# Another way to spread silu(c) over the partitions, in the first microseconds of a hybrid mixer layer

## The chip, the cores and the metric

The kernel runs on one core of a Trainium2 chip. The metric is device time in microseconds (us) of one execution. A core has five engines that run beside each other and meet through semaphores: TensorE (PE, matrix products), VectorE (DVE), ScalarE (ACT), GpSimd (POOL) and SyncE (SP), and 16 DMA engines that move the data that SP, ACT and POOL ask for.

## The reference

One decoder layer on 1024 tokens of 1024 features, all in fp32. Cut to what matters here:

```python
c_act = silu(c)                                   # c has 1024 values
mod = c_act @ mod_w + mod_b                       # 1024 x 3072
shift, scale, gate = split(mod, 3)
h = rmsnorm(x, norm_g) * (1 + scale) + shift
u = h @ w_in                                      # 1024 x 5120: five parts
cv, cg, cs, lx, ls = split(u, ...)
y_conv = (silu(layernorm(conv31(cv * sigmoid(cg)))) @ pw2_w + pw2_b) * silu(cs)
y_lru = linear_scan(gates of conv4(lx)) * silu(ls)
x = x + (1 + gate) * (concat(y_conv, y_lru) @ w_out)
return rmsnorm(x, final_g)
```

Nothing of h can be computed before scale is known, and scale needs silu(c) times a third of mod_w.

## The kernel before

The features lie on the 128 partitions, in 8 tiles k = 0 to 7; the tokens lie along the free dimension. Large products are made of fp32r parts: an operand is cast to a high part (ACT) and the rest is formed by a subtraction (DVE, or POOL for some weights), and three products of such parts stand for one product: high times high, high times low, low times high.

**The opening.** All small vectors (biases, gains, c) come in one tile V, loaded by SP before everything else (L413). ACT makes cs = silu(c), 128 x 8 values. DVE needs silu(c) as a row that lies on every partition, since it forms scale as sums over the free dimension of mod_w's transposed rows. PE spreads it: `spread_c` (L724) multiplies, for each k, an identity with the column k of cs broadcast as weights, so that 128 columns of c_row receive the 128 values of that column on all partitions. Two PSUM tiles c_row0 and c_row1 hold four columns' worth each. These are fp32 products. Before and after them PE does filler products with `ones` (`idle_mm`, L721; IDLE = 12 in all, IDLE0 = 4 of them ahead of the spread). The two PSUM tiles come from the pool "mm" of three, of which the first output tiles also take theirs.

`first_dot` (L819) forms the first 128 values of scale from the two halves of c_row directly, in two products with modw on DVE, and adds the first half's sum into b1; after each, ACT copies that half of c_row to the buffer sc in SBUF, which later dots read. Then DVE forms gs = (sum + b) * norm_g, and with it uh = x * gs as the high part and ul as the low part.

**The first tiles.** Four output tiles of W_in (FIRST) are computed with k outermost, as x, mod_w and w_first arrive: for each k, a load of mod_w, of the first weights (`fraw`), of x; a dot; the cast of fraw to fhi (ACT), flo (DVE); uh and ul; products "first" on PE. The token statistics (squares of x) are summed beside it, and at the end PE sums them (token_stats), ACT takes the root, DVE the reciprocal st, PE spreads it with the identity, and ACT copies that to rbc, which scales the four tiles when DVE takes them out of PSUM (first_u). One half of the fourth tile has no room in PSUM at first and is computed afterwards ("late"), in the buffer of 512 columns that the other half of that tile leaves. The next three tiles (NEXT; "ps" and then DVE's "next") use the same unscaled uh and ul; their weights are cast on ACT to whi and completed on POOL as wlo. Beside this DVE works on shift (dots with mod_w, then "shift") and on its share of the bias (fsum).

**What sets the order.** Every operation is recorded with an engine, a cost, a priority, what it reads and writes. `Plan.order` simulates the five engines with these costs, picks on each free engine the ready operation of lowest priority number, and so writes one order by hand for each queue; the hardware then runs each engine in that order, with waits where data is needed. An operation's changed cost or priority can thus move others. Lines called helpers below: L345 and L353 are all of ACT's copies and activations, L364, L372 and L386 DVE's (and L372 POOL's) operations, L391 SP's loads. Operations called outside the plan (V's load, the identity, the memsets) come first on their engines. SP0 is the time at which the plan lets SP start.

Of the kernel before, what the change touches and what calls it, by code (L numbers as in the profile page):

```python
# [9 lines left out]
F32 = mybir.dt.float32  # L10
F32R = mybir.dt.float32r
AF = mybir.ActivationFunctionType
ALU = mybir.AluOpType

P = 128
D = 1024
T = 1024
KT = D // P
H = 512
# [8 lines left out]
DWW = SCW + KT * STAPS  # L28
# [4 lines left out]
FW = len(FIRST) * P  # L33
# [40 lines left out]
WARM = (2, 1)  # L74
LANDING, MARGIN = 4.0, 2.0
BACKLOG = 6.0
SP0 = 1.0
SPP = 35
PAD = 16
GLO = "DVE"  # L80
# [220 lines left out]
def hymba_layer(ctx: ExitStack, tc: tile.TileContext, xT, vecs, mod_w, w_first, w_in,  # L301
                gate_w, pw2, w_out, out):
    nc = tc.nc
    ctx.enter_context(tc.manual_schedule())
    act, dve, pool, pe, sp = nc.scalar, nc.vector, nc.gpsimd, nc.tensor, nc.sync

    const = ctx.enter_context(tc.tile_pool(name="const", bufs=1))
# [19 lines left out]
    S = Plan(pools)  # L327
# [11 lines left out]
    def ACT(prio, out, in_, func, n=T, bias=None, scale=None, accum=None, r=(), w=(),  # L339
            reserve=0, after=()):  # L340
        kw = {}

        def emit():
            if func == "copy":
                act.copy(out(), in_())  # L345
                return
            if bias is not None:
                kw["bias"] = bias
            if scale is not None:
                kw["scale"] = scale  # L350
            if accum is not None:
                kw["accum_out"] = accum
            act.activation(out=out(), in_=in_(), func=func, **kw)  # L353
        ptr = sum(x is not None and not isinstance(x, float) for x in (bias, scale))
        return S.op("ACT", a_cost(n, ptr) + (0.1 if accum is not None else 0), emit, prio, r, w,
                    table=SETS.get(func), reserve=reserve, after=after)
# [42 lines left out]
    def big_buf(name, dt=F32, parts=1):  # L399
        return S.buf("big", name, dt, parts)  # L400
# [9 lines left out]


    V = const.tile([P, NVEC], F32, tag="V", name="V")
    sp.dma_start(V[:, :DWW], vecs[:, :DWW])  # L413

    def vec(name, t):
        o = OFF[name] + t
        return V[:, o:o + 1]

    ident = const.tile([P, P], F32, tag="ident", name="ident")
    make_identity(nc, ident)  # L420
    ones = const.tile([P, P], F32, tag="ones", name="ones")
    dve.memset(ones, 1.0)
    ones_d = const.tile([P, P], F32, tag="ones_d", name="ones_d")
# [89 lines left out]
    def half(b, i):  # L513
        return part(b, i * H, i * H + H)
# [191 lines left out]

    xt = [big_buf(f"x{k}", parts=4) for k in range(KT)]
    sc = big_buf("sc", parts=2)  # L710
    psf = [mm_tile(f"first{n}", 4) for n in range(3)] + [acc_tile("first3")]
# [5 lines left out]
    cs, ps_c = ctile("cs", KT), [mm_tile(f"c_row{z}") for z in (0, 1)]  # L717
# [3 lines left out]
    def idle_mm():  # L721
        pe.matmul(psb()[:, :P], ones, ones, start=True, stop=True)

    def spread_c(z):  # L724
        for k in range(4 * z, 4 * z + 4):
            pe.matmul(half(ps_c[z], 0)()[:, k % 4 * P:k % 4 * P + P], cs[:, k:k + 1].to_broadcast([P, P]), ident,
                      start=True, stop=True)
    for i in range(IDLE):
        if i == IDLE0:
            for z in (0, 1):  # L730
                spread_op = S.op("PE", 0.11 * KT, lambda z=z: spread_c(z), -130, [("cs", 0)],
                                 [ps_c[z]], columns=2 * P * KT)
        S.op("PE", 0.22, idle_mm, -120, [], [psb], columns=4 * P,
             after=[spread_op] if i >= IDLE0 else [])
    def mod_load(j, prio, after=(), reserve=0):
# [16 lines left out]
    def fw_part(b, k, a=0, e=FW):  # L752
        o = (k % 2) * FW
        return lambda: b()[:, o + a:o + e]
# [24 lines left out]
    for i, ld in enumerate(LOADS):  # L779
        p = due[ld] = i - 100.0  # L780
        k = int(ld[1])
        if ld[0] == "s":
            mod_load(KT + k, p, reserve=RES)
        elif ld[0] == "h":
            mod_load(k, p, reserve=RES)
        elif ld[0] in "wW":
            nk = 1 + (ld[0] == "W")
            rw, hi, lo = fw[k - k % 2]
            n, o, js = nk * FW, (k % 2) * FW, range(k % 2, k % 2 + nk)
            keys = lambda b: [(b, j) for j in js]  # L790
            DMA(p, part(rw, o, o + n), lambda k=k, j=nk: w_first[k * P:(k + j) * P, :].rearrange(
                "(p j) f -> p (j f)", j=j), n * P * 4, w=keys(rw))
            for j in range(k, k + nk):
                due[f"w{j}"] = p
                jj = j % 2
                p += 1.5 * (j > k)
                ACT(p, fw_part(hi, j), fw_part(rw, j), "copy", FW, r=[(rw, jj)], w=[(hi, jj)])
                low[j] = SUB(p, "DVE", fw_part(lo, j), fw_part(rw, j), fw_part(hi, j), FW,
                             r=[(rw, jj), (hi, jj)], w=[(lo, jj)])
        else:  # L800
            if ld[0] == "a":
                due["x0"] = p
            for z in {"a": (0,), "b": (1,)}.get(ld[0], (0, 1)[:1 + (k == 0)]):
                x_load(p, xt[k], k, z)
# [30 lines left out]
    for k in range(KT):  # L835
        p = due[f"s{k}"]
# [3 lines left out]
        else:  # L840
            dot(SCALE[k], p, KT + k, [gs_op])
        gs_op = S.op("DVE", 0.2, lambda k=k, a_=a_: dve.scalar_tensor_tensor(
            out=col(gs, k), in0=a_, scalar=col(b1, k), in1=vec("norm_g", k), op0=ALU.add,
            op1=ALU.mult), p, [("macc", KT + k), ("b1", 0)], [("gs", k)], lock=True)
        p = max(p, due[f"x{k}"], due[f"w{k}"])
# [4 lines left out]
        for a, e in START if k < UK else ((0, T),):  # L850
            n = e - a
            hk = halves(x_, a, e)
            if k == 0 == a:
                o = first_u = TS(p, part(uh, a, e), part(x_, a, e), g, None, ALU.mult, n=n,
                       r=hk + [("gs", k)], w=halves(uh, a, e))
            else:
                o = ACT(p, part(uh, a, e), part(x_, a, e), AF.Copy, n, scale=g,
                        r=hk + [("gs", k)], w=halves(uh, a, e))
# [3 lines left out]
                r=hk + halves(uh, a, e) + [("gs", k)], w=halves(ul, a, e)))  # L862
# [3 lines left out]
        for ch, z in ((ch, z) for ch in (0, 1) for z in range(3 if k < ZK else 0)):  # L866
            for i, ps in enumerate(psf):
                if START[ch] in cuts[i]:
                    o = fw_mm(p + 0.1 * ch, ps, i, uh, ul, k, START[ch:ch + 1], z=z)
                    last_u[k, i, ch] = o  # L870
        for ch, (a, e) in enumerate(START):
            for i, ps in enumerate(psf):
# [3 lines left out]
                o = fw_mm(q, ps, i, uh, ul, k, ((a, e),))  # L876
# [3 lines left out]
    for k in range(KT):  # L880
        p = SQP + k
# [3 lines left out]
        for i, j in SQPAIR.get(k, ()):  # L885
            a, b = sqs[i], sqs[j]
# [21 lines left out]
    for a, e in START:  # L908
# [3 lines left out]
                         w=halves(rbc, a, e))  # L912
# [7 lines left out]
    for k in range(KT):  # L920
        p = due[f"h{k}"]
# [3 lines left out]
            out=col(shift, k), in0=a_, in1=vec("mod_shift_b", k), op=ALU.add), p,  # L925
            [("macc", k)], [("shift", k)], lock=True)
        rw = fw[k - k % 2][0]
        if k == 0:
            ACT(p, facc, fw_part(rw, k), AF.Copy, FW, scale=shift[:, k:k + 1],
                r=[(rw, 0), ("shift", k)], w=[(fsum, 0)])  # L930
# [3 lines left out]
        for i, s in enumerate(NEXT):  # L934
            to, rw = part(fsum, FW + i * P, FW + i * P + P), raw[s]
            src = lambda rw=rw, k=k: k3(rw)()[:, k, :]
            if k == 0:
                ACT(p + 5, to, src, AF.Copy, P, scale=shift[:, k:k + 1],
                    r=[(rw, k), ("shift", k)], w=[(fsum, 1)])
            else:  # L940
                STT(p + 5, to, src, shift[:, k:k + 1], to, ALU.mult, ALU.add, P,
                    r=[(rw, k), ("shift", k), (fsum, 1)], w=[(fsum, 1)])
    psx = mm_tile("psbias", 2)

    def shift_mm():
# [5 lines left out]
        w=[("bias", 0)])  # L951

    hh, hl = uhs, uls

    for ch, (a, e) in enumerate(START):
        for k in range(KT):
            p, n = TP + k + HCH * ch, e - a
# [57 lines left out]
    v, c = {}, {}  # L1015
# [210 lines left out]
    for i, (s, ps) in enumerate(zip(FIRST, psf)):  # L1226
        j, p, bi = s[1] % KT, EVP + i, bias[:, i:i + 1]
        t = big_buf(f"first_u{i}", parts=4)
        for a, e in START:
            tk, pk, n = halves(t, a, e), halves(ps, a, e), e - a  # L1230
# [3 lines left out]
            else:  # L1234
                late = acc_tile("late")
                for k in range(KT):
# [3 lines left out]
                   r=[late] + halves(rbc, a, e), w=tk)  # L1240
# [13 lines left out]
    n, started, acc_d = 3, {}, {}  # L1254
    for s in slots[4:]:
# [10 lines left out]
        ps = mm_tile(f"ps{n}")  # L1266
# [5 lines left out]
        for k in range(KT):  # L1272
            o = mm_k(n, ps, s, xh, xl, k, FULL)
# [13 lines left out]
        else:  # L1287
            t = big_buf(f"acc{m}")
            for z in (0, 1)[:1 + (m == 0)]:
                x_load(n - 1, t, m, z, [started[n - 2]])  # L1290
            STT(n + 0.5, t, ps, gate1[:, m:m + 1], t, ALU.mult, ALU.add,
                r=[ps, t, ("gate1", m)], w=[t])
# [7 lines left out]
    begun_pw2, last = [], [started[n - 1], started[n]]  # L1300
    for p in range(KT // 2):
        n = C0 + 2 * p
        w = pair_weights("pw2", p, n, last[:1], last[1:], WPW[p])
        ops, found = next(pair_products(f"pw2_{p}", n, w, v_sets, PW7[p]))
        begun_pw2.append(ops)
        last = [ops[0], ops[3]]
# [22 lines left out]
    acc, n = {}, D0  # L1329
# [163 lines left out]
```

## Time and profile before

| | us |
|---|---|
| median of 3 runs | 735.97 |
| lowest and highest | 735.59 and 736.16 |
| profiled execution, span from first to last instruction | 734.5 |
| PE busy in the span | 725.2 |
| DVE busy | 626.0 |
| ACT busy | 445.7 |
| POOL busy | 139.3 |

The page of the profile gives the profiled execution by its span alone; the median of the runs is 1.5 us longer than that. A busy time counts instructions from start to end; products on PE overlap, so 99% busy does not mean that it does as much as it could, only that it hardly waits. Rows of a timeline give the start in us from the span's start, the length, the engine, the line, the operation with out<-in, the shape and a count; brackets hold the idle time of the engine ahead of it and what ended it.

### The profile page before, as it was taken

The page shows a single profiled execution, that of the slowest core. Times are in us where ns is not written, and L with a number is a line of the kernel's source. Part 1 is how long each engine was busy: PE and PEld are TensorE (multiplying, and loading weights), DVE is VectorE, ACT ScalarE, POOL GpSimd, SP SyncE. Part 2 cuts the span into 40 slices and gives each one's busy share as a digit, 9 for nine tenths or more (in the row PEclk, how much of TensorE's full clock was granted, in tenths as well). Part 3 has the DMA queues.
Part 4 walks back from the last instruction along what each step waited for, and adds up shares of the span by engine and source line. Part 5 has one row for each costly group of instructions (what it writes and reads, how often), then busy time and mean ns, then how long its engine had stood idle before and what let it go on. Part 6 is the DMA issues. An engine that isn't in the chain of part 4 may idle for free.

```text
span 734.5 us, 8866 instructions
## 1 busy us (share of the span) xinstructions
PE 725.2 (99%) x3280; PEld 602.5 (82%) x3280; DVE 626.0 (85%) x834; ACT 445.7 (61%) x564; POOL 139.3 (19%) x125
## 2 busy tenths in 40 slices
PE   9999999999999999999999999999999999999996
PEld 8888888888888887888888888878888888888885
DVE  6999999999569996888598999849699766999756
ACT  7650677556679759957849788524664324565522
POOL 0024012344424222232214111310000000000003
PEclk9999999999999999999999999999999999999998
DMA  9951023458898999899654645634232530523306
GB/s 347 406 217 58 0 87 79 89 115 193 187 211 193 240 250 216 169 232 210 142 112 98 146 85 142 197 133 167 92 115 85 202 115 2 187 93 121 115 1 229
DMA packets 37483, 111.58 MB, mean 152 GB/s; under 512 B 4160, under 2 KB 12864, under 8 KB 37440
## 3 DMA queue, kind: packets, MB, share of 16 engines
q1 hardware_dynamic: 23904, 75.84, 29.7%
q0 software_dynamic: 12528, 34.26, 25.5%
q10 hardware_dynamic: 1008, 0.92, 0.4%
q8 instruction: 25, 0.41, 0.2%
q14 instruction: 18, 0.15, 0.1%
HBM read 64.16 MB, written 12.58 MB: 104 GB/s over the span
## 4 chain that ended last, share of the span: by engine, by line
PE 80%; DVE 12%; issue 3%; ACT 3%; DMA 2%; POOL 0%; DVEq 0%; SPq 0%; ACTq 0%; POOLq 0%
PE ps L489 54%; PE xpw L611 6%; PE xout L611 4%; PE ypw L611 3%; PE out L662 3%; DVE caccs L364 2%; DVE modw L364 2%; PE gate L1171 2%; PE yout L611 2%; PE zpw L611 1%; DVE ul L364 1%; DVE cacc L364 1%; PE zout L611 1%; DVE o L364 1%; DMA oo<-co 1%
## 5 line engine op out<-in xcount | busy, mean ns | idle before, releaser
L489 PE MATMUL ps<-uh,whi 128*128 128x512 f32 x576 | 177.4, 389 | 0.3 <-ACT scs L353 0.3
L489 PE MATMUL ps<-uh,wlo 128*128 128x512 f32 x576 | 177.4, 389 | 0.0
L489 PE MATMUL ps<-ul,whi 128*128 128x512 f32 x576 | 177.4, 389 | 0.0
L489 PEld LDWEIGHTS ps<-uh,whi 128*128 128x128 f32 x576 | 107.9, 188 | 23.0 <-ACT scs L353 0.7
L489 PEld LDWEIGHTS ps<-uh,wlo 128*128 128x128 f32 x576 | 108.1, 188 | 22.6
L489 PEld LDWEIGHTS ps<-ul,whi 128*128 128x128 f32 x576 | 108.1, 188 | 22.4
L345 ACT CAST whi<-raw 128x1024 fp32r<-128x1024 f32 x46 | 48.0, 1047 | 73.7 <-PE ps L489 45.3
L377 POOL DMA_DIRECT2D es<-cq x45 | 41.6, 946 | 124.6 <-ACT cq L353 92.7
L372 POOL TENSOR_TENSOR wlo<-raw,whi 128x1024 fp32r<-128x1024 f32 x16 | 40.1, 2515 | 125.9 <-ACT whi L345 85.1
L353 ACT ACT_TABLE_LOAD x45 | 57.7, 1283 | 4.9 <-DMA oo<-co 3.4
L364 DVE SCALAR_TENSOR_TENSOR cacc<-v,V,cacc 128x511 f32<-128x511 f32 (+14 forms) x75 | 55.8, 744 | 0.5
L364 DVE SCALAR_TENSOR_TENSOR caccs<-v,V,caccs 128x511 f32<-128x511 f32 (+6 forms) x70 | 52.2, 745 | 2.4 <-ACT caccs L353 1.1
L364 DVE SCALAR_TENSOR_TENSOR caccs<-c,wsum,caccs 128x511 f32<-128x511 f32 (+6 forms) x70 | 52.1, 744 | 1.0
L372 POOL TENSOR_TENSOR o<-fin,bc 128x256 f32<-128x256 f32 (+1 forms) x7 | 6.0, 889 | 244.8 <-ACT bc L345 244.8
L377 POOL DMA_DIRECT2D oo<-co x42 | 38.2, 955 | 65.1 <-ACT co L353 23.2
L372 DVE TENSOR_TENSOR wlo<-raw,whi 128x1024 fp32r<-128x1024 f32 x30 | 38.5, 1284 | 9.9 <-ACT whi L345 9.9
L489 PE MATMUL ps<-yh,whi 128*128 128x512 f32 x128 | 40.0, 394 | 0.0
L489 PE MATMUL ps<-yl,whi 128*128 128x512 f32 x128 | 39.5, 390 | 0.0
L489 PE MATMUL ps<-yh,wlo 128*128 128x512 f32 x128 | 39.4, 389 | 0.0
L353 ACT ACTIVATE cq<-v,V 128x511 f32<-128x511 f32 (+14 forms) x45 | 31.8, 707 | 0.0
L364 DVE SCALAR_TENSOR_TENSOR xs<-ps,V,xs 128x1023 f32<-128x1023 f32 (+2 forms) x24 | 30.7, 1277 | 0.0
L364 DVE SCALAR_TENSOR_TENSOR modw<-modw,sc 128x1024 f32<-128x1024 f32 x23 | 30.1, 1311 | 0.0
(334 smaller groups left out, 1449.7 us busy)
## 6 DMA issues: line engine op xcount, KB each, us to landing
raw<-in_w_in_dram SPq DMA_DIRECT2D x36, 512.0 KB, 4.8
modw<-in_mod_w_dram SPq DMA_DIRECT2D x24, 512.0 KB, 8.1
raw<-in_w_out_dram SPq DMA_DIRECT2D x10, 512.0 KB, 4.0
scsd<-scs SPq DMA_DIRECT2D x8, 512.0 KB, 4.2
accd<-acc SPq DMA_DIRECT2D x8, 512.0 KB, 2.8
rawpw<-in_pw_dram SPq DMA_DIRECT2D x8, 512.0 KB, 3.5
scsr<-scsd SPq DMA_DIRECT2D x8, 512.0 KB, 5.8
fin<-accd SPq DMA_DIRECT2D x8, 512.0 KB, 4.8
```

Of the source, the lines that this page charges most:

```text
L345: act.copy(out(), in_())
L353: act.activation(out=out(), in_=in_(), func=func, **kw)
L364: dve.scalar_tensor_tensor(out=out(), in0=in0(), scalar=scalar, in1=in1(), op0=op0, op1=op1, accum_out=accum)
L372: lambda: e.tensor_tensor(out=out(), in0=a(), in1=b(), op=op), prio, r, w,
L377: return S.op("POOL", ISSUE, lambda: pool.dma_start(out(), a(), accum_op=ALU.add), prio, r, w, lag=RATE * n / T, after=after)
L489: pe.matmul(ps()[:, a - off:b - off], k3(lhs)()[:, k, :], rhs[k]()[:, a:b], start=(k == 0 and lhs is wh and rhs is xh and (a - off) % H == 0),
L611: pe.matmul(half(ps, 0)(), half(*lhs)()[:, j * P:j * P + P], half(*rhs)(), start=start and j == 0 and t == 0, stop=j == KT // 2 - 1 and t ...
L662: pe.matmul(ps()[:, a - off:e - off], k3(lhs)()[:, k, :], rhs()[:, i * H + a % H:i * H + a % H + e - a], start=k == KORD[0] and lhs is wh ...
L1171: pe.matmul(ps()[:, c0:c1], lhs()[:, j, :], rhs()[:, c0:c1], start=st == 0, stop=st == 2)
```

## The change

Four things change.

- V is loaded by a DMA that ACT issues, not SP; SP's first DMA is now the first piece of mod_w. The planner's SP0 goes from 1.0 to 0.6.
- The identity is a tile of type fp32r. POOL makes an identity in a large buffer, and DVE copies it. The fp32 uses read the same tile through a view.
- cs is split on DVE into csh (its fp32r cast) and csl (the rest). The spread multiplies the fp32r identity with csh and then with csl, summed in PSUM: 16 fp32r products in place of 8 fp32 products.
- The cast of the first weights (fhi for k = 0) gets the priority -101.5, ahead of ACT's copies of c_row to sc.

```diff
-SP0 = 1.0
+SP0 = 0.6
...
-    sp.dma_start(V[:, :DWW], vecs[:, :DWW])
+    act.dma_start(V[:, :DWW], vecs[:, :DWW])
...
-    ident = const.tile([P, P], F32, tag="ident", name="ident")
-    make_identity(nc, ident)
+    ident_r = const.tile([P, P], F32R, tag="ident", name="ident")
+    ident = ident_r.bitcast(F32)
+    made = big_buf("made")
+    S.op("POOL", 1.0, lambda: make_identity(nc, made()[:, :P]), -150, [], [made])
+    S.op("DVE", 0.2, lambda: dve.tensor_copy(ident_r, made()[:, :P]), -150, [made],
+         [("ident", 0)])
...
+    def two_parts(name, full, r, prio):
+        n = full.shape[-1]
+        hi, lo = (const.tile([P, n], F32R, tag=name + z, name=name + z) for z in "hl")
+        S.op("DVE", 0.15, lambda: dve.tensor_copy(hi, full), prio, r, [(name + "h", 0)])
+        S.op("DVE", 0.15, lambda: dve.tensor_tensor(
+            out=lo, in0=full, in1=hi.bitcast(F32), op=ALU.subtract), prio,
+            [*r, (name + "h", 0)], [(name + "l", 0)], lock=True)
+        return hi, lo
+
+    def spread_two(ps, hi, lo, ks, o):
+        k0 = ks[0]
+        for c, last in ((hi, False), (lo, True)):
+            for k in ks:
+                a = o + (k - k0) * P
+                pe.matmul(ps()[:, a:a + P], c[:, k:k + 1].to_broadcast([P, P]), ident_r,
+                          start=a % H == 0 and not last, stop=last, skip_group_check=True)
...
+    csh, csl = two_parts("cs", cs, [("cs", 0)], -130)
+
     def spread_c(z):
-        for k in range(4 * z, 4 * z + 4):
-            pe.matmul(half(ps_c[z], 0)()[:, k % 4 * P:k % 4 * P + P], cs[:, k:k + 1].to_broadcast([P, P]), ident,
-                      start=True, stop=True)
+        spread_two(lambda: half(ps_c[z], 0)(), csh, csl, range(4 * z, 4 * z + 4), 0)
     for i in range(IDLE):
         if i == IDLE0:
             for z in (0, 1):
-                spread_op = S.op("PE", 0.11 * KT, lambda z=z: spread_c(z), -130, [("cs", 0)],
-                                 [ps_c[z]], columns=2 * P * KT)
+                spread_op = S.op("PE", 0.06 * KT, lambda z=z: spread_c(z), -130,
+                                 [("csh", 0), ("csl", 0), ("ident", 0)], [ps_c[z]], columns=P * KT)
...
-                ACT(p, fw_part(hi, j), fw_part(rw, j), "copy", FW, r=[(rw, jj)], w=[(hi, jj)])
+                ACT(p if j else -101.5, fw_part(hi, j), fw_part(rw, j), "copy", FW, r=[(rw, jj)], w=[(hi, jj)])
```

What the planner makes of it, read from the two programs: ACT begins with V's load, then its first table load; its first cast of fraw comes ahead of both copies to sc. DVE's add of the first half's sum to b1 comes after the second half's product. Some flo, ul and sq operations change places between 16 and 40 us. On ACT the table load for the root comes ahead of fsum, and the first cast of NEXT weights (whi) after the first copy to rbc. On DVE the first_u operations come earlier among shift and fsum, and the softplus steps later. On POOL the wlo of the first NEXT tile is the third operation, not the second. On PE the sums of squares come one group of three products earlier among the "first" products, and the spreading of st moves among them. On SP two mod_w loads change places with weight loads. From about 100 us on the order is the same on every engine.

## Prediction

> **What bounds the kernel now.** I read the page's head first, then the waits of TensorE over the whole span, then the timeline of each engine over the first 60 us.
>
> ```profile
> span 734.5 us, 8866 instructions
> PE 725.2 (99%) x3280; PEld 602.5 (82%) x3280; DVE 626.0 (85%) x834; ACT 445.7 (61%) x564; POOL 139.3 (19%) x125
> ...
> PE token_stats L722 <- DVE ones L422: 1.1, 1, 1.1
> PE finbc L690 <- DVE rs64.5_0_5690 L699: 0.9, 1, 0.9
> PE late L765 <- DVE first_u L372: 0.8, 1, 0.8
> PE ps L489 <- ACT scs L353: 0.3, 1, 0.3
> ```
>
> TensorE (PE) waits four times in 734.5 us, 3.1 us in all. So only three things can move the end: work that PE does before its first useful product, one of these waits, or a new wait. The changed program has the same order on every engine after about 100 us, so I look at the first 60 us and take what PE has gained or lost there as carried to the end.
>
> ```profile
> 1.06 2.08 PE L722 MATMUL token_stats<-ones 128*128 128x128 f32 x8 [1.06 <-DVE ones L422]
> 3.00 3.75 PE L726 MATMUL c_row<-ident,cs 128*128 128x128 f32 x16
> 6.54 2.13 PE L722 MATMUL token_stats<-ones 128*128 128x128 f32 x16
> 8.43 1.17 PE L765 MATMUL first<-uh,fhi 128*128 128x512 f32 x4
> ...
> 41.19 1.84 PE L894 MATMUL token_stats<-ones,sq 128*128 128x1 f32 x16
> 42.89 0.49 PE L765 MATMUL first<-uh,fhi 128*128 128x512 f32 x1
> ```
>
> Columns: start, length, engine, line, tiles, count. The spread c_row is 8 fp32 products, shown as 16 passes: (6.54-3.00)/16 = 0.221 us each. The 16 filler passes after it need (8.43-6.54)/16 = 0.118. Later fp32 passes need (42.89-41.19)/16 = 0.106. So PE begins at half pace; with n filler passes at 0.221 and the rest at 0.106, n is 1.7, and full pace comes near 6.9 us. From 8.43 to 50.45 PE never waits.
>
> **The start, part by part.**
>
> ```profile
> 0.74 0.37 SPq L413 DMA_DIRECT2D V<-in_vecs_dram  x1
> 1.17 0.42 SPq L391 DMA_DIRECT2D modw<-in_mod_w_dram  x1
> ...
> 0.74 1.28 ACT L353 ACT_TABLE_LOAD   x1 [0.74 <-PEq L1485]
> 2.65 0.21 ACT L353 ACTIVATE cs<-V 128x8 f32<-128x8 f32 x1 [0.63 <-DMA V<-in_vecs_dram]
> 5.78 0.21 ACT L353 ACTIVATE sp_u<-sp_u 128x8 f32<-128x8 f32 x1
> 5.90 0.57 ACT L345 COPY sc<-c_row 128x512 f32<-128x512 f32 x1
> 6.36 0.62 ACT L345 CAST fhi<-fraw 128x512 fp32r<-128x512 f32 x1
> ...
> 2.65 0.17 DVE L386 TENSOR_SCALAR b<-V 128x16 f32<-128x16 f32 x1 [1.50 <-DMA V<-in_vecs_dram]
> 6.79 0.69 DVE L364 SCALAR_TENSOR_TENSOR modw<-modw,c_row 128x512 f32<-128x512 f32 x1 [0.82 <-PE c_row L726]
> 7.52 0.22 DVE L842 SCALAR_TENSOR_TENSOR gs<-macc,b,V 128x1 f32<-128x1 f32 x1
> 7.78 0.49 DVE L386 TENSOR_SCALAR uh<-x,gs 128x512 fp32r<-128x512 f32 x1
> ```
>
> V's load. On ScalarE (ACT) it goes ahead of the table load: 0.74+0.37+1.28 = 2.39, before V's landing at 2.65, so the issue is hidden; if V landed before 2.39 it would cost up to the 0.37. SP's other loads start 1.17-0.74 = 0.43 earlier. What V loses by sharing the engines with a 512 KB load is between 0 and 1.28 us (rival below); I take 0, the row as it stands.
>
> Identity. POOL makes it in another buffer, and VectorE (DVE) copies 128x128 in about 0.17 in its 1.50 us idle time: hidden. Without that cover it is 0.17.
>
> Two parts. c_row now waits for one more small DVE operation, csh. One such step, gs to uh, takes 7.78-7.52 = 0.26, so c_row starts at 3.26. The second part, csl, runs under the first four products.
>
> One-pass products. There are still 16, now one per part. What one takes at half pace no row shows.
>
> ```profile
> 11.27 0.84 PE L765 MATMUL first<-uh,fhi 128*128 128x512 f32 x3
> 11.95 0.84 PE L765 MATMUL first<-uh,flo 128*128 128x512 f32 x3
> ...
> 718.14 0.28 PE L662 MATMUL out<-yhb,whi 128*128 128x256 f32 x1
> 719.09 0.28 PE L662 MATMUL out<-yhb,wlo 128*128 128x256 f32 x1
> ```
>
> fp32r products take 0.227 us for 512 columns (0.68/3) and 0.119 for 256 (8 products in 0.95). By that slope 128 columns take 0.065, at half pace (times 0.221/0.118 = 1.9) 0.12. From above, if the 16 weight loads set the pace, 0.221 as today. The nearest rows are the one-pass products, so I take 0.13: c_row is issued from 3.26 to 5.35, not to 6.54. [...]
>
> What follows. The second modw product started 6.79-6.54 = 0.25 after c_row; now 5.60. gs followed 0.73 after that start; now the one-element add to b, hidden before, lies between (0.13 with its wait): 6.46, and uh 6.72. uh led to PE's first product in 8.43-7.78 = 0.65: 7.37. The cast of fraw no longer stands behind a copy of sc and may start at 5.90, where the table loads end, and be done by 6.5. The two copies of sc follow, to about 7.6; PE's second and third product need those buffers, and start after that anyway.
>
> Filler. PE still has 16 filler passes between. From 5.35 to 6.9 it does 7 at 0.221, then 9 at 0.106: 7.87. So fillers set the start: 8.43-7.87 = **0.56 us gained**, and up to 1.06 (7.37) where full pace comes sooner.
>
> Can the rest follow? The loads run 0.43 earlier, and DVE runs 1.06 ahead of its old times. The reordered flo, ul and sq operations between 20 and 40 us cost nothing as long as PE has none to wait for there, as today.
>
> **The middle.**
>
> ```profile
> 49.40 1.05 PE L900 MATMUL token_stats<-ident,st 128*128 128x128 f32 x8
> 51.29 0.50 PE L765 MATMUL late<-uh,fhi 128*128 128x512 f32 x1 [0.84 <-DVE first_u L372]
> 57.79 0.62 PE L489 MATMUL ps<-uh,wlo 128*128 128x512 f32 x2
> ...
> 44.72 0.20 DVE L907 RECIPROCAL st<-st 128x8 f32<-128x8 f32 x1
> 47.34 2.37 DVE L924 TENSOR_TENSOR shift<-macc,V 128x1 f32<-128x1 f32 x1
> 50.56 1.87 DVE L372 TENSOR_TENSOR first_u<-first,rbc 128x512 f32<-128x512 f32 x3
> ...
> 45.78 1.03 ACT L345 CAST whi<-raw 128x1024 fp32r<-128x1024 f32 x1
> 47.52 0.59 ACT L345 COPY rbc<-token_stats 128x512 f32<-128x512 f32 x1 [0.71 <-PE token_stats L900]
> ...
> 46.89 2.81 POOL L372 TENSOR_TENSOR wlo<-raw,whi 128x1024 fp32r<-128x1024 f32 x1 [45.58 <-ACT whi L345]
> 53.09 10.26 POOL L372 TENSOR_TENSOR wlo<-raw,whi 128x1024 fp32r<-128x1024 f32 x4 [3.39 <-DVE first_u L372]
> ```
>
> PE's 0.84 us wait is for the first_u that empties first3's buffer. It starts at 50.56 because a one-column shift took 2.37 us: it began inside POOL's wlo (46.89 to 49.70) and ended with it. In the changed order that cast of whi stands behind rbc, so POOL starts at 47.52+0.59+1.03 = 49.1; and on DVE only two shifts, a 512 fsum, a modw dot and another fsum lie between the reciprocal and first_u: the work that today lies between the starts at 44.72 and 47.34, 2.6 us, and one shift more. In today's clock: ready at 47.4, rbc at 48.1, first0's first_u to 48.7, first3's to 49.4, before PE reaches late at 50.45. **0.84 us gained**, with 1.0 us in hand; the other end is 0.
>
> What is late next: the wlo of the first NEXT tile (ps from 56.89). It was POOL's second wlo and becomes its third. POOL takes 10.26/4 = 2.57 each: 49.1 to 51.9, 54.5, 57.1; PE needs it where it now starts the wlo products, at 57.79-0.84 = 56.95. Wait 0.15, more where DVE holds POOL up; between 0 and 1.0 for a first reading I take **0.3 lost**.
>
> Sum: 0.56+0.84-0.30 = 1.1 us. The span becomes 733.4. The median of the runs, 735.97, lies 1.5 us above the profiled span; I keep that and forecast **734.9 us**. A measurement of this kernel tells about 0.2%, 1.47 us, from no change, so this stands just inside.
>
> **Rivals.**
> More gain: full pace comes within c_row and POOL does not stop PE: 1.06+0.84 = 1.9, 734.1. For it: the moment of full pace is not tied to this work by any row. Against: the profile has it at 6.9.
>
> V late. Today its packets have the engines first. If one 512 KB load passes first, V lands 1.28 later:
>
> ```profile
> 10.33 0.33 SPq L391 DMA_DIRECT2D x<-in_xT_dram  x1
> 11.61 0.33 SPq L391 DMA_DIRECT2D modw<-in_mod_w_dram  x1
> ...
> out_dram<-o ACTq DMA_DIRECT2D x7, 128.0 KB, 2.1
> ```
>
> (SP's issues here come one landing apart.) c_row runs 4.54 to 6.6, the fillers end near 8.5 and ACT's copies, 1.28 later, hold the third product to 8.9: PE about 0.3 later than today; 735.97+0.3-0.84+0.3 = 735.7. Against it: at the end ACT's stores land in 2.1 us beside SP's. [...]
>
> Weight loads bind (0.221 each): c_row ends 6.80, second modw 7.05, PE at 8.82, 0.39 later than today; 735.8.
>
> Half pace lasts: the thinner products do not count as the same activity. If it lasts one more stretch as long as c_row today, 3.5 us, to 10.4, the fillers end at 5.35+3.54 = 8.89 and half of the 1.5 us to 10.4 is lost: PE 1.2 later, 736.6. [...]
>
> Slower: POOL's third wlo. Today its second stood 3.39 us for work of others. If the third stands as long, it ends at 60.5 and PE waits 3.5 us in the first NEXT tile: 735.97-1.4+3.5 = 738.1. It decides from an end past 58.4 (today's clock). Against: two operations now pass first, and its inputs are older by then.
>
> **How the numbers follow.** Forecast 734.9 (own range 734.2 to 735.6) 0.43, of which 0.12 lies under 734.5; more gain 0.26; V late 0.09; weight loads 0.07; half pace 0.05; POOL 0.10. Faster by over 0.2%: 0.12+0.26 = 0.38; slower 0.10; within 0.52. The low end is the second case with 0.5 us of room, 733.6; the high end, 736.4, leaves out POOL and half of the half-pace case.
>
> **What would show it.** c_row at 16 passes of 0.12 to 0.14 us, cs still at 2.65, first at 7.4 to 7.9, no wait of late, a wait under 0.6 us at the first wlo of ps, and the same distance between PE's later landmarks as before. Wrong: cs after 3.0, c_row passes near 0.22, fillers at 0.22 past 7 us, or PE waiting anew at ps, gate or scs.

## The result, and the profile after

The changed kernel takes 738.84 us (median of 5 runs, 737.47 to 739.18), the kernel before 735.97 (5 runs beside them, 735.37 to 736.53). The ratio is 1.0037, with a 95% interval of 1.0026 to 1.0048: 0.37% slower, where 0.15% faster was forecast. The profiled execution has a span of 737.03 us, 2.57 more than before, and is itself the run of 738.84. One execution of the experiments below, of the one-pass filler around an fp32 spread, had a granted clock of 0.751 over its span and took 915.01 us; its ratio leaves it out.

First the timelines of the changed kernel for ScalarE (ACT), VectorE (DVE) and TensorE (PE), and the loads of the first 8 us (queue, KB, us from issue to landing).

```profile
0.74 0.42 ACTq L413 DMA_DIRECT2D V<-in_vecs_dram  x1
1.19 1.28 ACT L353 ACT_TABLE_LOAD   x1 [1.19 <-PEq L1506]
5.12 0.21 ACT L353 ACTIVATE cs<-V 128x8 f32<-128x8 f32 x1 [2.65 <-DMA V<-in_vecs_dram]
...
5.36 0.17 DVE L716 CAST csh<-cs 128x8 fp32r<-128x8 f32 x1 [3.79 <-ACT cs L353]
...
5.59 1.12 PE L727 MATMUL c_row<-ident,csh 128*128 128x128 f32 x4 [2.46 <-DVE csh L716]
6.50 1.05 PE L727 MATMUL c_row<-ident,csl 128*128 128x128 f32 x4
7.36 1.05 PE L727 MATMUL c_row<-ident,csh 128*128 128x128 f32 x4
8.21 1.05 PE L727 MATMUL c_row<-ident,csl 128*128 128x128 f32 x4
9.06 3.72 PE L743 MATMUL token_stats<-ones 128*128 128x128 f32 x16
12.44 1.46 PE L786 MATMUL first<-uh,fhi 128*128 128x512 f32 x4
...
V<-in_vecs_dram ACTq DMA_DIRECT2D x1, 72.0 KB, 4.4
```

Before, the same landmarks stood at 2.65 (cs), 3.00 (spread), 6.54 (filler passes) and 8.43 (first product). PE's first product is now 4.01 us later, and four numbers make that up. V landed 2.47 late (5.12 - 2.65). csh lies between: cs to spread is 0.47, was 0.35, so +0.12. The 16 spread passes take 9.06 - 5.59 = 3.47, were 3.54: -0.07. The 16 filler passes take 12.44 - 9.06 = 3.38, or 0.211 each, were 1.89: +1.49. PE is still at half pace when the first product starts; the trace's record of the granted clock has full pace from 13.06 us, and from 6.92 in the kernel before. (The trace has no earlier record of it; that PE runs at half pace until then is read from the passes, 0.21 us each ahead of that moment and 0.11 behind it.)

The waits of PE over the whole span (us in total, times, longest), and the chain of work through the first 70 us of the changed kernel (start, length, what):

```profile
PE c_row L727 <- DVE csh L716: 2.5, 1, 2.5
PE token_stats L743 <- DVE ones L426: 1.1, 1, 1.1
PE finbc L694 <- DVE rs64.5_0_5704 L703: 0.9, 1, 0.9
```

```profile
0.74 4.36 DMA V<-in_vecs_dram
5.12 0.22 ACT cs L353
5.36 0.18 DVE csh L716
5.59 3.68 PE c_row L727 x16
9.27 3.52 PE token_stats L743 x16
```

The wait of `late` for first_u (0.8) is gone, and the wait for csh is new. The wait of ps for scs (0.3) is missing too, but the change did not remove it: it sits near 287 us, and with the order of before it is there in the kernel before and not with V alone on ACT, with the changed order it is not here and there with V on SP. V's load, which was nowhere near the end before, now heads the chain. Of the 4.01 us, 3.33 are left at `late` (54.62, was 51.29). The way there from the first product is 42.18, was 42.86, although the first four products, still at half pace, take 0.3 more (1.30, was 1.01): the order saves 1.0 on it, the wait of 0.84 included. At the end of the span 2.6 remain: the difference is still 3.2 up to the wait of ps for scs near 287 us, and 2.6 right behind it.

### The profile page after: what moved, and what is told of

It is laid out like the page before. It is cut to its first block, busy times and chain, and to the rows that moved or that the text cites. A ratio compares the mean times of both kernels' runs of the same rounds, so it can differ in the third digit from the quotient of the medians.

```text
span 737.0 us, 8863 instructions
## 1 busy us (share of the span) xinstructions
PE 726.5 (99%) x3280; PEld 604.1 (82%) x3280; DVE 625.3 (85%) x837; ACT 446.3 (61%) x564; POOL 139.6 (19%) x125
## 4 chain that ended last, share of the span: by engine, by line
PE 97%; DVE 1%; DMA 1%; ACT 0%; DVEq 0%; issue 0%
PE ps L493 65%; PE xpw L615 6%; PE first L786 5%; PE xout L615 4%; PE gate L1192 3%; PE ypw L615 3%; PE out L666 3%; PE yout L615 2%; PE zpw L615 1%; PE zout L615 1%; DVE o L364 1%; PE late L786 1%; DMA V<-in_vecs_dram 1%; PE c_row L727 0%; PE token_stats L743 0%; PE vout L615 0%
## 5 line engine op out<-in xcount | busy, mean ns | idle before, releaser
L364 DVE SCALAR_TENSOR_TENSOR modw<-modw,sc 128x1024 f32<-128x1024 f32 x23 | 33.8, 1477 | 0.0
```

Of the source, the lines that this page charges most:

```text
L364: dve.scalar_tensor_tensor(out=out(), in0=in0(), scalar=scalar, in1=in1(), op0=op0, op1=op1, accum_out=accum)
```

## The experiments

Two questions: why is V late, and why does full pace come late? The second had two theories. TIME: PE stood idle until 5.59, and nothing else matters. THIN: a one-pass product of 128 columns occupies PE but does not bring full pace. "Kernel before" ratios below are to runs of it on the same chip.

The trace's records of full pace, from the first to the last moment, last 716.80, 720.21 (changed kernel), 723.63 (kernel before) or 727.04 us in these executions: steps of 3.41 us. I read that as a pace that is granted or not in stretches of 3.41 us, an estimate from these lengths alone. Full pace begins between 4.72 and 14.67 us in these executions, and these moments are not whole steps of 3.41 apart, so the place of the stretches is not tied to the kernel's start. Each execution thus has some luck in it, and times are compared by medians. Below, the stretches of an execution are counted back from its moment of full pace; one that ended without full pace is called refused.

### V back on SP

```diff
-    act.dma_start(V[:, :DWW], vecs[:, :DWW])
+    sp.dma_start(V[:, :DWW], vecs[:, :DWW])
```

> The changed kernel with one edit: SP issues V's load again, ahead of its big loads. Every engine's order is else that of the changed kernel. Theory QUEUE (V is late because ACT's queue shares the transfer engines with SP's big loads): V lands 1.9 us after its issue again, cs at 2.65 instead of 5.12, c_row at about 3.12 (cs + 0.47). Rival HEAD (V is late for another reason, for instance that so many transfers start at once): cs stays near 5.1 and the time near 738.8. On the pace of the filler passes two theories: TIME (full pace was late only because PE stood idle from 3.1 to 5.6): the 16 spread passes take 3.5 us to 6.6, the 16 filler passes 1.9 as before, first product at 8.5, and with the late wait of 0.84 and the ps wait of 0.3 gone 735.97 - 1.14 + 0.1 = 734.9. THIN (the one-pass products do not bring PE to full pace): the filler passes take 3.4 us, first product at 10.0, + 1.6 and 0.3 for the first products, so 735.97 - 1.14 + 1.9 = 736.7.

Measured: 736.50 us, ratio 1.0004 (0.9995 to 1.0013). PE's timeline, and one of its waits:

```profile
3.12 1.12 PE L727 MATMUL c_row<-ident,csh 128*128 128x128 f32 x4
...
6.59 3.25 PE L743 MATMUL token_stats<-ones 128*128 128x128 f32 x16
9.60 1.16 PE L786 MATMUL first<-uh,fhi 128*128 128x512 f32 x4
...
PE ps L493 <- ACT scs L353: 0.3, 1, 0.3
```

cs is back at 2.65 (HEAD falls), so V's lateness is a matter of the queue. PE has no gap from 1.06 us on and yet the filler passes take 3.01 us; full pace comes at 9.21. TIME fails and THIN's 736.7 was near. The wait of ps for scs, which the expectation had counted as gone, is back, at 288 us.

### The same, with the fp32 products of before

The order of every engine and the copies csh and csl stay those of the changed kernel.

```diff
-        spread_two(lambda: half(ps_c[z], 0)(), csh, csl, range(4 * z, 4 * z + 4), 0)
+        for k in range(4 * z, 4 * z + 4):
+            pe.matmul(half(ps_c[z], 0)()[:, k % 4 * P:k % 4 * P + P], cs[:, k:k + 1].to_broadcast([P, P]), ident,
+                      start=True, stop=True)
```

> The changed kernel with two parts undone: SP issues V's load, and the spread is made by the 8 fp32 products of before (cs and ident, 16 passes of 0.221). The copies csh and csl and the order of all engines stay as in the changed kernel. So only the order (the first cast ahead, the late wait) and the wait for csh and csl remain of the change. Spread from 3.1 to 6.6, filler passes 1.9, first product 8.5 under TIME and THIN alike; 735.97 - 0.84 (late) - 0.3 (ps) + 0.1 = 734.9; 735.2 if the ps wait returns. Its difference from the kernel with V on SP and the one-pass products is the price of the form: 0 under TIME, + 1.8 for the one-pass form under THIN. Rival ORDER (the late wait only moves to another place): 735.9 to 736.1.

Measured: 735.11 us, ratio 0.9986 (0.9977 to 0.9995). This version is faster than both kernels. PE's timeline:

```profile
2.93 3.46 PE L749 MATMUL c_row<-ident,cs 128*128 128x128 f32 x16
6.23 1.95 PE L743 MATMUL token_stats<-ones 128*128 128x128 f32 x16
8.12 1.17 PE L788 MATMUL first<-uh,fhi 128*128 128x512 f32 x4
```

The spread is as long as the one-pass spread (3.30 against 3.47), but the filler passes behind it take 1.89, not 3.01, and full pace is there at 5.96. These two kernels differ in the form of the spread alone, and by 736.50 - 735.11 = 1.39 us. What is left of the change, its order above all, gains 735.93 - 735.11 = 0.82 (0.4 to 1.7 by the interval) against the 735.93 of the kernel before on this chip; the expectation had 735.2 for the case that ps waits for scs again, as it does (0.3).

### Only V's load moved

The kernel before, with V issued by ACT and nothing else.

```diff
-    sp.dma_start(V[:, :DWW], vecs[:, :DWW])
+    act.dma_start(V[:, :DWW], vecs[:, :DWW])
```

> The kernel before with one edit: ACT issues V's load. Every engine's order is else that of the kernel before; the spread has its fp32 products. QUEUE: V lands 4.4 us after its issue, cs at 5.1, PE idle from 3.1 to about 5.45, the 16 spread passes to 9.0. HEAD: cs at 2.65 and 735.97. THIN: fp32 products bring full pace within 4 us of 5.45, so the filler passes take 1.9 to 2.3 us, the first product comes at 11.0 to 11.3 and the time is 735.97 + 2.6 to 2.9 = 738.6 to 738.9. TIME: the idle gap alone delays full pace, the filler passes take 3.4 us as in the changed kernel, first product at 12.4, time 735.97 + 4.0 + 0.3 = 740.3. The late wait of 0.84 stays under all.

Measured: 738.97 us, ratio 1.0033 (1.0020 to 1.0045). ACT's and PE's timelines, and a wait:

```profile
5.08 0.21 ACT L353 ACTIVATE cs<-V 128x8 f32<-128x8 f32 x1 [2.61 <-DMA V<-in_vecs_dram]
...
8.98 2.76 PE L722 MATMUL token_stats<-ones 128*128 128x128 f32 x16
11.49 1.17 PE L765 MATMUL first<-uh,fhi 128*128 128x512 f32 x4
...
PE late L765 <- DVE first_u L372: 0.2, 1, 0.2
```

This one line costs as much as the whole change. V lands 4.3 us after its issue; PE is idle until 5.43, and fp32 passes then bring full pace at 10.67, in time for part of the filler (2.51 us). The time agrees with what THIN gave. `late` waits 0.2 here, not 0.8; why was not tried.

### The gap filled

The changed kernel, V on ACT, with six more filler products ahead of the spread, so that PE works from 1.06 to 5.3.

```diff
-        S.op("PE", 0.22, idle_mm, -120, [], [psb], columns=4 * P,
-             after=[spread_op] if i >= IDLE0 else [])
+        S.op("PE", 0.22, lambda n=7 if i == IDLE0 - 1 else 1: [idle_mm() for _ in range(n)],
+             -120, [], [psb], columns=4 * P, after=[spread_op] if i >= IDLE0 else [])
```

> The changed kernel, V on ACT as there, with 6 more filler products ahead of the spread, so that PE runs from 1.06 to about 5.4 without a gap until the spread starts at 5.59. Nothing else moves. TIME: full pace near 6.9 as before or earlier, the last 8 or more of the 16 one-pass products run at full pace and show what one costs there: 0.106 if it is paced by its weight load as an fp32 pass is, 0.065 if by its columns; c_row done by 8.0 to 8.2, the 16 filler passes 1.7, then the first product waits for uh, at about 9.9: + 1.5 at the start, with 1.14 gained later 736.3. THIN: the fillers ahead bring full pace, but the one-pass products lose it again, so that the filler passes behind them take 2 to 3.4 us: first product 10.5 to 12.4, time 737 to 738.8.

Measured: 736.03 us, ratio 1.0002 (0.9991 to 1.0013), so 2.81 us less than the changed kernel, with V at least as late as there (cs at 5.50). Nine of the ten runs lie between 735.76 and 736.16; the tenth took 739.79, and no profile of it shows why. PE's timeline and weight loads (PEld), and from the kernel before the fp32 products that spread st at full pace (shortest, median and longest of one in ns):

```profile
1.06 4.23 PE L743 MATMUL token_stats<-ones 128*128 128x128 f32 x20 [1.06 <-DVE ones L426]
5.96 0.66 PE L727 MATMUL c_row<-ident,csh 128*128 128x128 f32 x4 [0.68 <-DVE csh L716]
6.46 0.61 PE L727 MATMUL c_row<-ident,csl 128*128 128x128 f32 x4
6.91 0.61 PE L727 MATMUL c_row<-ident,csh 128*128 128x128 f32 x4
7.36 0.61 PE L727 MATMUL c_row<-ident,csl 128*128 128x128 f32 x4
7.80 2.00 PE L743 MATMUL token_stats<-ones 128*128 128x128 f32 x16
9.70 1.41 PE L786 MATMUL first<-uh,fhi 128*128 128x512 f32 x4
...
6.41 0.53 PEld L727 LDWEIGHTS c_row<-ident,csl 128*128 128x128 f32 x4
...
L900 PE MATMUL token_stats<-ident,st x16: 271/275/275, 46.4 to 50.2; 128*128 128x128 f32 x16
```

Full pace is there at 4.72 and the one-pass products keep it. Here one costs (6.91 - 6.46)/4 = 0.112 us at full pace, and its weight loads overlap without a gap. An fp32 pass of 128 columns costs as much there: the prediction's row at 49.40 has 8 of them in 1.05 us, the last one 0.275 long, so (1.05 - 0.275)/7 = 0.111 from one to the next. (The prediction's 0.106, from its row at 41.19, is of fp32 passes of one column, 128x1 in the row; in the trace these too start 0.112 apart.) At half pace single passes of both forms start 0.213 apart in the trace; the 0.221 and 0.217 of whole rows hold their edges. So the one-pass form gains nothing at either pace, and at full pace an fp32 pass costs the same with 1 column as with 128. The first product stands at 9.70, 1.27 later than before, though V is 2.85 later: the earlier full pace makes up the rest.

### Fewer filler products

V on SP, one-pass spread, and 4 filler products behind the spread in place of 8.

```diff
-IDLE, IDLE0 = 12, 4
+IDLE, IDLE0 = 8, 4
```

> The changed kernel with V on SP and 4 filler products (8 passes) instead of 8 (16 passes) behind the spread. Nothing else moves. Compared with the run that has V on SP and all fillers (736.5; spread to 6.59, filler passes to 9.60 nearly all at half pace, full pace at 9.2). THIN, with useful products lifting the pace as well as fillers do: 8 passes of 0.21 end at 8.3, where uh is ready (8.2 to 8.3), so the first products start at 8.35 and run at half pace for about 1 us: 1.25 - 0.5 = 0.75 gained, 735.75. Rival NEED (the pace waits for the fillers' number, not for PE's work): full pace later by as much as the fillers save, 736.4 to 736.6. Rival HOLE (PE now stands idle before the first product and full pace goes late): 737 or more.

Measured: 736.13 us, ratio 1.0000 (0.9991 to 1.0010), 0.37 less than with all fillers. The two were run on different chips and scatter enough (735.54 to 736.90 and 735.44 to 737.96) that this is not a clear difference. PE's timeline:

```profile
8.65 2.04 PE L786 MATMUL first<-uh,fhi 128*128 128x512 f32 x4
10.49 1.30 PE L786 MATMUL first<-uh,flo 128*128 128x512 f32 x4
```

The first product starts 0.95 earlier, but its four take 1.84 instead of 1.00 because full pace comes at 10.94. The run lies between its expectations, and settles nothing.

### All one-pass before the first product

V on SP and the one-pass spread, and each filler product made of two one-pass fp32r products of ones.

```diff
-    ones = const.tile([P, P], F32, tag="ones", name="ones")
+    ones_r = const.tile([P, P], F32R, tag="ones", name="ones")
+    ones = ones_r.bitcast(F32)
...
-        pe.matmul(psb()[:, :P], ones, ones, start=True, stop=True)
+        for _ in range(2):
+            pe.matmul(psb()[:, :P], ones_r, ones_r, start=True, stop=True)
```

> The run with V on SP and the one-pass spread (736.5; full pace at 9.2), with one edit: each fp32 filler product becomes two one-pass fp32r products, so that before the first product PE runs nothing but one-pass products of 128 columns. The number of passes is the same. THIN: no full pace before the first product at 10.0; the 512-column products bring it 2 to 4 us later, at 11.5 to 14; the time is 0.4 for the start and about 1 for the slow products above the 736.5: 737.4 to 738.2. TIME: PE is busy from 1.06 on, so full pace is there by 4.5 to 8, one-pass products after it take 0.112, first product by 8.5, 735.0 to 735.4. Neither: as the run it is made from, 736.3 to 736.7, if only the spread's products are at fault.

Measured: 738.10 us, ratio 1.0029 (1.0019 to 1.0038). PE's timeline:

```profile
7.22 3.62 PE L745 MATMUL token_stats<-ones 128*128 128x128 f32 x16
10.64 2.02 PE L788 MATMUL first<-uh,fhi 128*128 128x512 f32 x4
12.45 1.91 PE L788 MATMUL first<-uh,flo 128*128 128x512 f32 x4
```

PE is busy from 1.06 on but for 0.72 us, and full pace comes at 14.67, after one whole stretch of 512-column products. Of the two stretches refused before it, the first (4.43 to 7.84) held one-pass products of 128 columns without a gap and nothing else. TIME fails. THIN's time holds, though full pace comes later than its 11.5 to 14. In this execution V was also later (spread at 3.75), which is 0.6 of the first product's delay.

### One-pass filler around an fp32 spread

The kernel of 735.11 with the same edit of the filler alone.

> The kernel with V on SP and the fp32 spread (735.11; full pace at 5.96), with one edit: each filler product, fp32 and two passes, becomes two one-pass fp32r products of the same ones. The number of passes and their length at half pace (0.21 to 0.22) are the same. THIN (a one-pass product of 128 columns keeps PE less than fully busy and does not bring full pace): only the spread from 2.9 to 6.2 counts, so full pace comes at 5.9 to 7.5 where a moment of granting falls there and otherwise only with the first products, at 11 to 13; median time 736.1 to 736.8, with more scatter. TIME (any pass counts): as the kernel it is made from, 734.9 to 735.3.

Measured: 735.29 us, ratio 0.9991 (0.9982 to 1.0000): as the kernel it is made from, so the 736.1 to 736.8 that I derived from THIN is wrong. The profile is of a second run of the same kernel:

> The kernel with V on SP, the fp32 spread and one-pass filler products again, for a profile. Its 735.29 was far below the 736.1 to 736.8 that THIN had been given there. If THIN holds with a bound of about half (a stretch of 3.4 us counts when more than about two thirds of it are fp32 or full products), the spread's 3.3 us at 2.9 to 6.2 are enough by themselves: full pace at 5.5 to 8.0 in this profile too, filler passes of 0.11 behind it, time 734.9 to 735.9.

Measured: 735.13 us; full pace at 8.36. PE's timeline:

```profile
2.95 3.78 PE L751 MATMUL c_row<-ident,cs 128*128 128x128 f32 x16
6.38 2.92 PE L745 MATMUL token_stats<-ones 128*128 128x128 f32 x16
9.14 1.14 PE L790 MATMUL first<-uh,fhi 128*128 128x512 f32 x4
```

The stretch before full pace, 4.94 to 8.36, held 1.44 us of fp32 passes and 1.97 of one-pass products. So one-pass products seem to count for something: in the kernel before, the stretch from 0.09 to 3.50 held 2.44 us of fp32 passes and nothing else, and was refused. Set beside the other executions: the last stretch refused was one-pass work of 128 columns for 83% (changed kernel), 78% (V on SP), 76% (fewer fillers) and 82% (all one-pass), the rest of it fp32 passes or products of 512 columns; here a stretch with 58% of them brought full pace. But the stretch before it, 1.53 to 4.94, with 42%, was refused, though PE had no gap in it, and that contradicts any simple share. How much a one-pass product counts, and why, stays open; that a stretch mostly of them was not enough was seen four times.

### Why V is late: c ahead in a smaller load

The kernel before with V on ACT, V in two loads.

```diff
-    act.dma_start(V[:, :DWW], vecs[:, :DWW])
+    act.dma_start(V[:, OFF["c"]:DWW], vecs[:, OFF["c"]:DWW])
+    act.dma_start(V[:, :OFF["c"]], vecs[:, :OFF["c"]])
```

> The kernel before with V on ACT, and V cut in two loads there: c and its neighbours first (128 packets of 160 bytes), the other 416 bytes of each partition behind it. Theory TURNS (on each transfer engine V's packets take turns with SP's, one small packet for one of 4096 bytes): the number of packets ahead is as before, so c lands as late as all of V did, cs at 4.9 to 5.1. Rival BYTES (the two queues share by bytes, or V only waits for its own size): c lands in about 160/576 of the extra time, cs at 3.2 to 3.5. Time 738.5 to 739.5 under TURNS, 736.5 to 737.5 under BYTES.

Measured: one run, 737.71 us. Loads of the first 8 us, and ACT's timeline:

```profile
V<-in_vecs_dram ACTq DMA_DIRECT2D x1, 52.0 KB, 4.5
V<-in_vecs_dram ACTq DMA_DIRECT2D x1, 20.0 KB, 4.1
...
4.84 0.21 ACT L353 ACTIVATE cs<-V 128x8 f32<-128x8 f32 x1 [1.90 <-DMA V<-in_vecs_dram]
```

20 KB take 4.1 us, 72 KB took 4.3. The bytes of the small load hardly matter: BYTES falls. That its 128 packets do is seen in the next trace. The time is 1.26 less than with V in one load, but both are within what the place of the stretches moves (full pace came at 8.35, not 10.67).

### Why V is late: smaller packets beside it

The kernel before with V on ACT in one load, and SP's first 128 x 1024 loads halved.

```diff
+            if prio < -90 and i.shape[-1] == T and len(o.shape) == 2:
+                sp.dma_start(o[:, :H], i[:, :H])
+                sp.dma_start(o[:, H:], i[:, H:])
+            else:
+                sp.dma_start(o, i)
...
```

> The kernel before with V on ACT, and SP's first loads of 128 x 1024 cut into two of 128 x 512, so that each of their packets has 2048 bytes. V itself is as in the run with V on ACT alone (cs at 5.08). TURNS: each of V's packets waits for half as much, so that half of the 2.4 us lost comes back: cs at 3.8 to 4.1. Rival BEHIND (V simply waits until the first big load, handed over at the same moment, is through): cs at 5.0 to 5.1 as before, since that load has as many bytes. Time 737.5 under TURNS, 739 under BEHIND.

Measured: one run, 737.63 us. Loads and ACT's timeline:

```profile
V<-in_vecs_dram ACTq DMA_DIRECT2D x1, 72.0 KB, 3.5
...
4.21 0.21 ACT L353 ACTIVATE cs<-V 128x8 f32<-128x8 f32 x1 [1.75 <-DMA V<-in_vecs_dram]
```

With packets of 2048 bytes beside it V lands at 4.2 instead of 5.1, though the bytes that SP hands over are the same for the opening. 0.87 of the 2.4 us lost come back, where TURNS had half. By itself this does not separate the two theories: the edit halves the first big load as well as its packets, and V behind a load of half the size would land earlier too. The trace of the run with V alone on ACT does separate them. These are its packets from 2.8 to 3.8 us, SP's queue (q1) and ACT's (q10; packets, MB, share of the engines' time):

```profile
q1 hardware_dynamic: 74, 0.30, 73.6%
q10 hardware_dynamic: 73, 0.04, 16.3%
```

Over all transfer engines together, V's packets of 576 bytes start one for one with modw's of 4096 bytes, and not when that load is through: BEHIND falls and TURNS holds. All 128 of them start between 2.46 and 4.50 us; in the kernel before they had all started by 2.26.

### The cast alone

The kernel before with only the last part of the change, the earlier cast.

```diff
-                ACT(p, fw_part(hi, j), fw_part(rw, j), "copy", FW, r=[(rw, jj)], w=[(hi, jj)])
+                ACT(p if j else -101.5, fw_part(hi, j), fw_part(rw, j), "copy", FW, r=[(rw, jj)], w=[(hi, jj)])
```

> The kernel before with only the change's third part: ACT casts the first fraw to fhi ahead of its first copy of c_row into sc. The order of all engines is else that of before (the planner's start of SP and its cost of the spread stay). Theory ORDER (the 0.8 us come from the order of late, first_u and the casts of wlo in the middle, which only the planner's numbers move): 735.7 to 736.2, and the wait of late for first_u stays at 0.8. Rival CAST (the earlier cast is what gains): first product earlier than 8.43 or the late wait gone, 735.0 to 735.4.

Measured: 735.87 us, ratio 1.0000 (0.9991 to 1.0009). One of PE's waits:

```profile
PE late L765 <- DVE first_u L372: 1.1, 1, 1.1
```

The cast gains nothing by itself and `late` still waits. The 0.82 us of the order thus lie elsewhere: PE goes from its first product to `late` in 42.86 us in the kernel before and in 41.89 in the kernel of 735.11, which has no wait there. Which of the planner's other numbers moved it was not tried one by one.

## Why the prediction was wrong, by its own steps

**V's load, "hidden, I take 0"**: the step that failed first. I checked only the issue on ACT (which is hidden: the table load was done at 2.47, V landed at about 5.1) and bounded the landing by one big load passing first, 1.28. What decided here was not bytes ahead but turns: V's packets and those of 4096 bytes went one for one (76 and 78 of them start between 2.8 and 3.8 us in the changed kernel), and V ended when that load did (last packets through at 4.61 and 4.56). The term is 2.47. The row I held against it, ACT's stores landing in 2.1 us late in the kernel, does not carry over to the opening; why those do not suffer was not tried. The rival "V late" had the right step, by one load that passes first, at half the size and at a chance of 0.09; it still forecast a gain (735.7).

**csh, 0.26**: 0.12 was added (cs to spread 0.47, was 0.35). **Identity, hidden**: right; DVE's copy stood in its idle time.

**One-pass products, 0.13 at half pace**: 0.217. I scaled a slope over columns down to 128, where it no longer holds: at full pace an fp32 pass takes 0.112 whether it has 1 column or 128. The upper bound, 0.221, was the value; that the weight load sets it fits this but was not tested apart.

**Full pace near 6.9, filler 7 slow and 9 fast**: it came at 13.06, all 16 slow. The 6.9 itself fits the record of the kernel before (6.92), by some luck, as the 0.106 in its working is of one-column passes. But I had carried the moment over as a time on the clock. In these traces it followed PE's work, in stretches of 3.41 us: the gap of 2.46 us and a stretch of one-pass products put it off. In place of 0.56 gained, the start lost 4.01. "Half pace lasts" had this at 1.2 and a chance of 0.05.

The rivals were each priced as if alone. They are not independent: V's lateness opens a gap, which together with the thin products moves the pace (full from 6.92 us before, 10.67 with V alone on ACT, 9.21 with V back on SP, 13.06 in the changed kernel). Filling the gap alone took back 2.81 us of the change's 2.87.

**The wait of `late`, 0.84 gained**: right; the wait is absent in every profile with the changed order and present, at 0.2 to 1.1, in those with the order of before that are shown here. The order by itself is worth 0.82. **POOL's third wlo, 0.3 lost**: it did not happen, PE has no wait at the first ps; POOL has that wlo done at 60.50 and PE takes it up at 60.99. The slower rival built on it (738.1) came near the time by luck. **What PE has lost by 60 us carries to the end**: nearly; 3.2 became 2.6, where the kernel before waits near 287 us.

**Level**: 735.93 before, beside the experiments, in steps of the medians: the order -0.82 (735.11), the one-pass form +1.39 (736.50), V on ACT +2.34 (738.84). Alone, V on ACT cost 3.0; what a step costs depends on the others, since V and the form both act through the one moment of full pace. Each step carries the scatter of its runs, several tenths of a us.

## What to carry to other kernels

Put a small load on which the first work hangs on the queue that also issues the big loads, ahead of them; on a second queue it shared turns with them here, packet by packet (73 to 74), and landed 4.3 us after its issue in place of 1.9; 20 KB fared hardly better (4.1). Before splitting an fp32 product into one-pass parts, compare the time of one pass: at 128 columns, with weights loaded for each, the two forms cost the same here (0.213 us at half pace, 0.112 at full), and the one-pass form delayed full pace (9.21 us, against 5.96). In the opening, price a PE gap not by its length but by when full pace then comes (with V alone on ACT PE had a gap of 2.30 us, and full pace came 3.75 later, at 10.67 against 6.92), and look for filler work that bridges it, as six products did here, for 2.81 us.

## What the runs showed of the hardware that I had not expected

- A 72 KB load of 128 packets landed 4.3 to 4.7 us after its issue beside another queue's packets of 4096 bytes, 3.5 beside packets of 2048, 1.9 to 2.0 when its packets went first (with all one-pass about 2.5, an estimate: the spread began 0.63 later there than with V on SP, 3.75 against 3.12); 20 KB in as many packets took 4.1.
- A pass of 128 columns with its own weight load, one-pass fp32r or one of the two of an fp32 product, starts 0.213 us after the one before it at half pace and 0.112 at full; an fp32 pass of one column needs 0.112 too.
- PE can be busy without a gap and stay at half pace: from 5.59 to 13.06 us in the changed kernel, from 1.06 to 9.21 with V on SP, with one-pass products of 128 columns in most of a stretch each time.
- With the gap filled, full pace once reached (4.72) was not lost by 1.8 us of one-pass products, nor by the gap of 0.68 ahead of them.
